# Two-layer hybrid block on one core: a shorter inverse square root, accumulating transfers for the low halves of the head weights, and a new order of the heads' products

## Chip, cores and metric

One core of a Trainium2 chip. The metric is the device time of one execution in microseconds (us); before the change three runs gave 2362.91, 2363.47 and 2366.34, median 2363.47.

## What is computed

Two layers (l = 0, 1), each of three sublayers on x of 512 positions by 1024 channels. All norms are root-mean-square norms with a gain per channel.

```python
for l in range(DEPTH):
    h = swiglu_ffn(rmsnorm(x, ffn1_pre_g[l]), ffn1_w_gu[l], ffn1_w_down[l])
    x = x + 0.5 * rmsnorm(h, ffn1_post_g[l])
    h = mixing_sublayer(rmsnorm(x, mix_pre_g[l]), w_in[l], ...)
    x = x + rmsnorm(h, mix_post_g[l])
    h = swiglu_ffn(rmsnorm(x, ffn2_pre_g[l]), ffn2_w_gu[l], ffn2_w_down[l])
    x = x + 0.5 * rmsnorm(h, ffn2_post_g[l])
```

`swiglu_ffn` is silu(h Wa) * (h Wb) times Wdown with 2816 hidden columns. `mixing_sublayer` multiplies h by a wide `w_in`, runs four branches (a gated MLP over chunks, window means, sparse attention, a causal convolution) and mixes them by gates and `w_out`. `rmsnorm` is h times rsqrt(mean(h*h) + 1e-6) times the gain.

## The kernel before

**Layout and precision.** x is held transposed, eight tiles of 128 channels by 512 positions. Every product of a weight w and a moving tile x is made from rounded high halves and the remainders, as three matmuls: wH·xH, wL·xH, wH·xL (`mm3s`, L244; the `matmul` is L256). So each weight needs two tiles of 128x1024, `wH` and `wL`, four buffers each, and each moving tile an `xH` and an `xL`.

**Weights** (`weights`, L179). A transfer on the SP queue brings the weight to `raw` (L183), the scalar engine (ACT) rounds it to `wH` (L196), and `wL` = raw - wH is made in one of three ways: on VectorE (DVE) by one subtraction (L205), on GpSimd (POOL) in two halves (L205 with `pool`; the first weight of a head has its own form, L189 and L190), or with `far`: ACT writes -wH to `wL` (L198) and a transfer on the POOL queue adds the weight out of DRAM onto it (L199). The mixers' `w_in`, `w_branch` and `w_out` weights use `far`, the feed-forward sublayers' gate, up and down weights use DVE.

**The boundary between two sublayers** (`boundary`, L408; five of them, three behind a feed-forward sublayer and two behind a mixer). The last four output tiles of a sublayer (its tail) and the first four weight columns of the next (its head) are worked in two halves of 256 positions, so that the norm in between overlaps with matmuls. TensorE's order is: tail of the low half, tail of the high half, head of the low half, head of the high half. During the high tail the norm of the low half runs, during the low head that of the high half:

- `compact` (L290): matmuls by a column of ones sum the squares (L296).
- `post_stats` (L346): a chain of small DVE instructions on 128x2 numbers gives the inverse root. Behind a feed-forward sublayer, which works on values not yet scaled by its own pre-norm, this is L357, L358, the eleven of `rsqrt` (L276, three Newton steps) and L360; behind a mixer L362 and the eleven. Two `diag` instructions (L304) put the result on diagonals.
- `spread` (L308): matmuls by ones (L312) bring it to every partition.
- `post_steps` (L377): per channel tile k, DVE scales (L387) and adds to x (L390; odd k on POOL in the high half), ACT makes `xH` (L395). Then eight DVE instructions make `xL` (L401), and ACT and POOL (low half) or DVE (high half) sum the squares for the next pre-norm (L440, L442).

Meanwhile `tail` (L543 and L727) takes each finished tail tile out of PSUM, squares it on ACT (L440) and adds the square to a running sum on DVE or POOL (L442), and `head_weight` (L478 and L563), called after each high tail tile, makes the next head weight; the three of them behind the first have POOL subtract.

**What sets the order.** `after` (L232) keeps a list of work due at a count of TensorE time; `mm3s` looks at it before each step of its own order. So `spread` is asked for 4300 ns of matmuls behind `compact`. The tile framework then schedules each engine's instructions by this program order and by its own estimate of when operands are ready; `pin` (L208) holds chosen ones to program order.

The head's four columns are one call of `mm3s` with `lag=2`:

```python
for ks in (range(n - 1), range(n - 1, n)):
    order += [(k - d, (o, 0)) for k in range(n + lag) for o, d in ((0, 0), (1, lag)) if k - d in ks]
    order += [(k, (0, 1)) for k in ks]
```

that is, for k below 7 the products wH·xH with wL·xH two steps behind, then wH·xL, then the three for k = 7; at each step all four columns. One half of a head is 96 matmuls.

Of the kernel before, what the change touches and what calls it, by code (L numbers as in the profile page):

```python
# [38 lines left out]
ACTIVE = 3  # L39

# [8 lines left out]
class Builder:  # L49
# [129 lines left out]
    def weights(self, src, n, pool=False, ring=False, raw=None, far=False):  # L179

        nc = self.nc
        raw = raw or self.t([P, 1024], F32, "raw", 2)
        nc.sync.dma_start(raw[:, :n], src)  # L183
        if ring:
            hs, ls = [], []
            for i in range(2):
                h, lo = self.ring(), self.ring()
                r = raw[:, i * N:(i + 1) * N]
                nc.scalar.activation(h, r, AF.Copy)  # L189
                nc.gpsimd.tensor_tensor(lo, r, h.bitcast(F32), op=ALU.subtract)  # L190
                hs.append(h)
                ls.append(lo)
            return hs, ls
        h = self.t([P, 1024], F32R, "wH", 4)
        lo = self.t([P, 1024], F32R, "wL", 4)
        self.pin(nc.scalar.activation(h[:, :n], raw[:, :n], AF.Copy))  # L196
        if far:
            nc.scalar.activation(lo[:, :n], raw[:, :n], AF.Copy, scale=-1.0)  # L198
            nc.gpsimd.dma_start(lo[:, :n], src, accum_op=ALU.add)  # L199
            return h, lo  # L200
        e = nc.gpsimd if pool else nc.vector
        w = N if pool and n > N else n
        for c in range(0, n, w):
            c = slice(c, min(c + w, n))
            self.pin(e.tensor_tensor(lo[:, c], raw[:, c], h.bitcast(F32)[:, c], op=ALU.subtract))  # L205
        return h, lo
# [37 lines left out]
    def mm3s(self, jobs, first=True, last=True, lag=0):  # L244

        n = len(jobs[0][1])
        order = []
        for ks in (range(n - 1), range(n - 1, n)):
            order += [(k - d, (o, 0)) for k in range(n + lag) for o, d in ((0, 0), (1, lag)) if k - d in ks]
            order += [(k, (0, 1)) for k in ks]  # L250
        for i, (k, (a, b)) in enumerate(order):
            self.run_due()
            for out, pairs in jobs:
                w, m = pairs[k]
                self.pe += m[b].shape[-1] / 2.4 + 2.5
                self.nc.tensor.matmul(out, w[a], m[b], start=(first and i == 0), stop=(last and i == 3 * n - 1))  # L256
# [12 lines left out]
    def gemms(self, outs, ws, mv, cs=FULL, n=2):  # L269

        for i in range(0, len(outs), n):
            self.mm3s([(o[:, slice(*cs)], self.pairs(w, mv, cs)) for o, w in zip(outs[i:i + n], ws[i:i + n])],
                      lag=2 if n == TAIL else 0)


    def rsqrt(self, y, v):  # L276
        nc = self.nc
        w = v.shape[-1]
        t = self.t([P, 8], F32, "s8", 8)[:, :w]
        nc.vector.tensor_scalar(t.bitcast(I32), v.bitcast(I32), 1, None, op0=ALU.logical_shift_right)  # L280
        nc.vector.tensor_scalar(y.bitcast(I32), t.bitcast(I32), -1.0, float(0x5f3759df), op0=ALU.mult, op1=ALU.add)
        for _ in range(3):
            nc.vector.tensor_tensor(t, y, y, op=ALU.mult)
            nc.vector.scalar_tensor_tensor(t, t, -0.5, v, op0=ALU.mult, op1=ALU.mult)  # L284
            nc.vector.scalar_tensor_tensor(y, t, 1.5, y, op0=ALU.add, op1=ALU.mult)
# [14 lines left out]
    def diag(self, r, cs):  # L300
        c0, c1 = cs[0] // P, cs[1] // P
        dg = self.tmp()
        for c in range(c0, c1):
            self.nc.vector.tensor_scalar(dg[:, c * P:(c + 1) * P], self.ident, r[:, c - c0:c - c0 + 1], None,  # L304
                                         op0=ALU.mult)
# [28 lines left out]
    def pre_stats(self, sub):  # L334
        nc = self.nc
        self.rc = self.t([P, 4], F32, "rc", 2)
# [4 lines left out]
        self.rsqrt(self.rc, ms)  # L341
        dg = self.diag(self.rc, FULL)
# [3 lines left out]
    def post_stats(self, sq, cs, half):  # L346

# [5 lines left out]
        if half:  # L353
            rc = self.rc_prev[:, c0:c0 + w]
            t = self.s8(w)
            nc.vector.tensor_tensor(t, rc, rc, op=ALU.mult)
            nc.vector.scalar_tensor_tensor(ms, ps, 1.0 / D, t, op0=ALU.mult, op1=ALU.mult)  # L357
            nc.vector.tensor_scalar(ms, ms, EPS, None, op0=ALU.add)  # L358
            self.rsqrt(r, ms)
            nc.vector.scalar_tensor_tensor(r, r, 0.5, rc, op0=ALU.mult, op1=ALU.mult)  # L360
        else:
            nc.vector.tensor_scalar(ms, ps, 1.0 / D, EPS, op0=ALU.mult, op1=ALU.add)  # L362
            self.rsqrt(r, ms)
        return self.diag(r, cs)

    def post(self, s, cs, nxt):
# [3 lines left out]
        self.after(4300, lambda: self.step(steps))  # L370
# [74 lines left out]
class FFN:  # L445
# [6 lines left out]
    def gu_weights(self, f, pool=False):  # L452
        return [self.b.weights(self.wgu[self.l, f, ab], 1024, pool) for ab in range(2)]
# [24 lines left out]
    def head_weight(self, i):  # L478
        if i < TAIL:
            self.hw.append(self.b.weights(self.wgu[self.l, i // 2, i % 2], 1024, True, raw=self.b.spare(i)))  # L480
# [20 lines left out]
    def rest(self):  # L501
        b, nc = self.b, self.b.nc
        b.rc_prev = b.rc
# [47 lines left out]
class Mix:  # L551
# [5 lines left out]
    def w(self, i, pool=False, raw=None, far=False):  # L557
        return self.b.weights(self.b.a["w_in"][self.l, i], 1024, pool, raw=raw, far=far)
# [4 lines left out]
    def head_weight(self, i):  # L563
        b = self.b
        if i < TAIL:
            self.hw.append(self.w(i, True, b.spare(i)))
# [220 lines left out]
    def gmlp(self, zv, u):  # L787
# [20 lines left out]
        b.rsqrt(r, ms)  # L808
# [30 lines left out]
    def conv(self):  # L839
# [20 lines left out]
        dg = b.diag(mu, FULL)  # L860
# [192 lines left out]
```

## Time and profile before

| | |
|---|---|
| median of three runs | 2363.47 us |
| the profiled execution's own time | 2364.17 us |
| its span in the profile | 2362.5 us |
| TensorE busy | 2289.8 us (97%) |
| VectorE, ACT, POOL busy | 1231.8, 917.3, 305.8 us |
| moved from DRAM | 270.46 MB, 115 GB/s over the span |

The span runs from the first instruction to the last. Engines are PE (TensorE's matmuls), PEld (its weight loads), DVE, ACT, POOL and SP; L312 is line 312 of the kernel. In a timeline a bracket at the end of a line gives the time that the engine sat idle before it and what ended that.

### The profile page before, as it was taken

Reading aid. Unit: us, or ns where it says so; the run is one execution under the profiler, and the core shown is the slowest. Engines: PE = TensorE matmul, PEld = TensorE weight load, DVE = VectorE, ACT = ScalarE, POOL = GpSimd, SP = SyncE. Lnnn points to the kernel's source line nnn. Section 1 sums busy time; section 2 is a strip of 40 time slices with the busy share of each in tenths; the row PEclk is TensorE's granted clock in tenths of the full one; section 3 lists DMA queues with packets and bytes.
Section 4 is the critical chain, followed back from the end, with each engine's and each line's share of the span. In section 5 each row is a group of like instructions: output and inputs, shape, how many; then the busy total and the mean of one; then the engine's idle time right before and its main releaser. Section 6 shows DMA issues by size and latency. Waiting matters only on the chain.

```text
span 2362.5 us, 28445 instructions
## 1 busy us (share of the span) xinstructions
PE 2289.8 (97%) x11158; PEld 1914.2 (81%) x11158; DVE 1231.8 (52%) x2226; ACT 917.3 (39%) x1375; POOL 305.8 (13%) x341
## 2 busy tenths in 40 slices
PE   8999998999999999999999999989999998999996
PEld 7888888777788888888888888887778888888886
DVE  5334347899433742433573333478985337424335
ACT  4222224564554432222333322345545544322221
POOL 0000003311331300000210000032123213000001
PEclk9999999999999999999999999999999999999998
DMA  5333321867777233333222333327677762333331
GB/s 167 98 106 89 107 89 54 187 143 175 177 163 176 81 100 97 96 101 95 89 83 87 109 96 100 97 64 170 143 178 176 172 160 72 108 92 92 102 93 60
DMA packets 80399, 274.41 MB, mean 116 GB/s; under 512 B 9189, under 2 KB 12937, under 8 KB 80265
## 3 DMA queue, kind: packets, MB, share of 16 engines
q1 hardware_dynamic: 64136, 213.87, 28.8%
q0 software_dynamic: 16128, 58.73, 14.7%
q8 instruction: 87, 1.43, 0.2%
q14 instruction: 48, 0.39, 0.0%
HBM read 270.46 MB, written 2.10 MB: 115 GB/s over the span
## 4 chain that ended last, share of the span: by engine, by line
PE 86%; DVE 8%; DMA 2%; issue 2%; ACT 1%; POOL 0%; SPq 0%; POOLq 0%; ACTq 0%; DVEq 0%
PE mm L256 53%; PE at L256 32%; DMA wL<-in_w_in_dram 1%; DVE x L390 1%; DVE ca L850 1%; DVE xL L401 1%; DVE t L387 1%; DMA raw<-in_w_in_dram 1%; PE st L312 1%; PE st L296 0%; PE at L954 0%; DVE t L304 0%; DVE sc L920 0%; DVE s L284 0%; DMA raw<-in_ffn_w_gu_dram 0%
## 5 line engine op out<-in xcount | busy, mean ns | idle before, releaser
L196 ACT ACTIVATE wH<-raw 128x1024 fp32r<-128x1024 f32 (+1 forms) x394 | 407.4, 1037 | 836.2 <-issue 556.4
L256 PE MATMUL mm<-xH,wH 128*128 128x512 f32 (+1 forms) x1504 | 566.6, 386 | 3.5 <-ACT wH L196 3.5
L256 PE MATMUL mm<-xH,wL 128*128 128x512 f32 (+1 forms) x1504 | 561.3, 383 | 7.9 <-DMA wL<-in_w_in_dram 7.9
L205 DVE TENSOR_TENSOR wL<-raw,wH 128x1024 fp32r<-128x1024 f32 (+1 forms) x272 | 324.2, 1194 | 231.7 <-ACT wH L196 231.6
L256 PE MATMUL mm<-h,wH 128*128 128x512 f32 (+1 forms) x1496 | 407.8, 353 | 0.9 <-DVE t L741 0.9
L256 PE MATMUL mm<-xL,wH 128*128 128x512 f32 (+1 forms) x1504 | 393.0, 379 | 0.0
L256 PEld LDWEIGHTS mm<-xH,wL 128*128 128x128 f32 x1504 | 280.5, 190 | 63.9 <-DMA wL<-in_w_in_dram 10.0
L256 PEld LDWEIGHTS mm<-xH,wH 128*128 128x128 f32 x1504 | 280.8, 191 | 61.2 <-ACT wH L196 4.5
L256 PEld LDWEIGHTS mm<-xL,wH 128*128 128x128 f32 x1504 | 278.2, 189 | 52.9
L256 PE MATMUL at<-xH,wH 128*128 128x512 f32 (+1 forms) x784 | 300.7, 385 | 7.4 <-ACT xH L226 7.2
L256 PEld LDWEIGHTS mm<-h,wH 128*128 128x128 f32 x1496 | 263.2, 188 | 42.2 <-DVE t L741 1.1
L256 PE MATMUL at<-xH,wL 128*128 128x512 f32 (+1 forms) x784 | 297.1, 380 | 0.0
L256 PE MATMUL mm<-h,wL 128*128 128x512 f32 (+1 forms) x748 | 253.8, 354 | 0.0
L256 PE MATMUL at<-h,wH 128*128 128x512 f32 (+1 forms) x776 | 219.6, 366 | 0.0
L256 PE MATMUL at<-xL,wH 128*128 128x512 f32 (+1 forms) x784 | 210.6, 378 | 0.0
L198 ACT ACTIVATE wL<-raw 128x1024 fp32r<-128x1024 f32 x112 | 118.2, 1055 | 185.9 <-PE mm L256 153.5
L256 PEld LDWEIGHTS at<-xH,wH 128*128 128x128 f32 x784 | 148.8, 190 | 37.9 <-ACT xH L226 7.5
L256 PEld LDWEIGHTS at<-xH,wL 128*128 128x128 f32 x784 | 148.4, 189 | 29.3 <-issue 1.4
L256 PEld LDWEIGHTS at<-xL,wH 128*128 128x128 f32 x784 | 147.5, 188 | 27.5
L256 PEld LDWEIGHTS at<-h,wH 128*128 128x128 f32 x776 | 140.4, 188 | 24.6
L256 PEld LDWEIGHTS mm<-h,wL 128*128 128x128 f32 x748 | 140.4, 188 | 20.5
L256 PE MATMUL at<-h,wL 128*128 128x512 f32 (+1 forms) x388 | 136.5, 366 | 0.0
(202 smaller groups left out, 2124.1 us busy)
## 6 DMA issues: line engine op xcount, KB each, us to landing
raw<-in_ffn_w_gu_dram SPq DMA_DIRECT2D x173, 512.0 KB, 3.6
raw<-in_w_in_dram SPq DMA_DIRECT2D x98, 512.0 KB, 6.3
wL<-in_w_in_dram POOLq DMA_DIRECT2D x88, 512.0 KB, 7.2
raw<-in_ffn_w_down_dram SPq DMA_DIRECT2D x64, 448.0 KB, 3.3
raw<-in_ffn_w_down_dram SPq DMA_DIRECT2D x32, 512.0 KB, 3.5
raw<-in_w_branch_dram SPq DMA_DIRECT2D x16, 512.0 KB, 5.2
wL<-in_w_branch_dram POOLq DMA_DIRECT2D x16, 512.0 KB, 7.2
raw<-in_w_out_dram SPq DMA_DIRECT2D x16, 512.0 KB, 5.9
```

Source lines behind the costliest of these rows:

```text
L196: self.pin(nc.scalar.activation(h[:, :n], raw[:, :n], AF.Copy))
L198: nc.scalar.activation(lo[:, :n], raw[:, :n], AF.Copy, scale=-1.0)
L205: self.pin(e.tensor_tensor(lo[:, c], raw[:, c], h.bitcast(F32)[:, c], op=ALU.subtract))
L256: self.nc.tensor.matmul(out, w[a], m[b], start=(first and i == 0), stop=(last and i == 3 * n - 1))
L312: self.nc.tensor.matmul(ps[:, s], self.ones, dg[:, s], start=True, stop=True)
L387: nc.vector.scalar_tensor_tensor(u[:, c], s.o[k][:, c], self.v(s.post[0], s.post[1] + k), pb[:, c], op0=ALU.mult, op1=ALU.mult)
L390: e.tensor_tensor(self.xt[k][:, c], self.xt[k][:, c], u[:, c], op=ALU.add)
L401: nc.vector.scalar_tensor_tensor(self.xl[k][:, c], self.xt[k][:, c], g, self.xh[k].bitcast(F32)[:, c], op0=ALU.mult, op1=ALU.subtract)
L850: nc.vector.scalar_tensor_tensor(a, hp[:, t:t + N], dw(t), a, op0=ALU.mult, op1=ALU.add)
```

## The change

- `rsqrt` starts from one instruction instead of two, makes one Newton step and one step of third order: eight instructions for eleven, with a constant factor of 0.375 left for `diag` to multiply in (or a ninth instruction, in the gated MLP).
- Behind a feed-forward sublayer the pre-norm's own factor is no longer divided out and put back: `pre_stats` keeps 1e-6 times its mean square plus 1e-6 (`ep`, one instruction behind its `diag`), and `post_stats` forms its argument in one instruction. From `compact` to `diag` there are nine small instructions where there were fourteen; behind a mixer nine where there were twelve.
- `spread` is asked for 3400 ns behind `compact` instead of 4300.
- The three later head weights use `far`: ACT writes -wH, the POOL queue issues an adding transfer. POOL's subtractions there are gone, and ACT's copy is pinned.
- The head's products are ordered by `heads`: wH·xH for all k and columns, wL·xH of the first three columns, wH·xL for all, and wL·xH of the last column. The list of due work is looked at before each matmul.

```diff
         if far:
-            nc.scalar.activation(lo[:, :n], raw[:, :n], AF.Copy, scale=-1.0)
+            self.pin(nc.scalar.activation(lo[:, :n], raw[:, :n], AF.Copy, scale=-1.0))
             nc.gpsimd.dma_start(lo[:, :n], src, accum_op=ALU.add)
...
+    def heads(self, jobs):
+        ks = range(KD)
+        js = range(len(jobs))
+        order = [(j, k, 0, 0) for k in ks for j in js]
+        order += [(j, k, 1, 0) for j in js[:-1] for k in ks]
+        order += [(j, k, 0, 1) for k in ks for j in js]
+        order += [(js[-1], k, 1, 0) for k in ks]
+        count = [0] * len(jobs)
+        for j, k, a, b in order:
+            self.run_due()
...
-        nc.vector.tensor_scalar(t.bitcast(I32), v.bitcast(I32), 1, None, op0=ALU.logical_shift_right)
-        nc.vector.tensor_scalar(y.bitcast(I32), t.bitcast(I32), -1.0, float(0x5f3759df), op0=ALU.mult, op1=ALU.add)
-        for _ in range(3):
-            nc.vector.tensor_tensor(t, y, y, op=ALU.mult)
-            nc.vector.scalar_tensor_tensor(t, t, -0.5, v, op0=ALU.mult, op1=ALU.mult)
-            nc.vector.scalar_tensor_tensor(y, t, 1.5, y, op0=ALU.add, op1=ALU.mult)
+        t, h = self.s8(v.shape[-1]), self.s8(v.shape[-1])
+        nc.vector.tensor_scalar(y.bitcast(I32), v.bitcast(I32), -0.5, float(0x5f3759df), op0=ALU.mult, op1=ALU.add)
+        nc.vector.tensor_tensor(t, y, y, op=ALU.mult)
+        nc.vector.scalar_tensor_tensor(t, t, -0.5, v, op0=ALU.mult, op1=ALU.mult)
+        nc.vector.scalar_tensor_tensor(y, t, 1.5, y, op0=ALU.add, op1=ALU.mult)
+        nc.vector.tensor_tensor(t, y, y, op=ALU.mult)
+        nc.vector.tensor_tensor(h, t, v, op=ALU.mult)
+        nc.vector.scalar_tensor_tensor(t, h, -10.0 / 3.0, h, op0=ALU.add, op1=ALU.mult)
+        nc.vector.scalar_tensor_tensor(y, t, 5.0, y, op0=ALU.add, op1=ALU.mult)
+        if exact:
+            nc.vector.tensor_scalar(y, y, CUBIC, None, op0=ALU.mult)
...
         if half:
-            rc = self.rc_prev[:, c0:c0 + w]
-            t = self.s8(w)
-            nc.vector.tensor_tensor(t, rc, rc, op=ALU.mult)
-            nc.vector.scalar_tensor_tensor(ms, ps, 1.0 / D, t, op0=ALU.mult, op1=ALU.mult)
-            nc.vector.tensor_scalar(ms, ms, EPS, None, op0=ALU.add)
-            self.rsqrt(r, ms)
-            nc.vector.scalar_tensor_tensor(r, r, 0.5, rc, op0=ALU.mult, op1=ALU.mult)
+            nc.vector.scalar_tensor_tensor(ms, ps, 1.0 / D, self.ep_prev[:, c0:c0 + w], op0=ALU.mult, op1=ALU.add)
...
-        self.after(4300, lambda: self.step(steps))
+        self.after(3400, lambda: self.step(steps))
...
-            self.hw.append(self.b.weights(self.wgu[self.l, i // 2, i % 2], 1024, True, raw=self.b.spare(i)))
+            self.hw.append(self.b.weights(self.wgu[self.l, i // 2, i % 2], 1024, raw=self.b.spare(i), far=True))
...
-            self.hw.append(self.w(i, True, b.spare(i)))
+            self.hw.append(self.w(i, b.spare(i), True))
```

## Rows read from the trace of the kernel before

**Rows 1.** Waits, in total, of TensorE's matmuls: us, times, longest us.

```profile
PE st L312 <- DVE t L304: 20.3, 9, 3.4
```

**Rows 2.** Windows over both halves of the head, first boundary and sum of five.

```profile
378.80:410.40 31.60, 27.29 (x208) 0.95 0.16 51
...
sum 157.70, PE 132.74; mean PE 26.55
```

**Rows 3.** Timeline of TensorE: sums (L296) and spreads (L312), first and third boundary, end.

```profile
374.14 0.70 PE L312 MATMUL st<-t,ones 128*128 128x256 f32 x2 [1.65 <-DVE t L304]
...
383.81 0.58 PE L296 MATMUL st<-ones,t 128*128 128x1 f32 x4 [1.66 <-DVE t L442]
...
394.48 0.70 PE L312 MATMUL st<-t,ones 128*128 128x256 f32 x2 [1.59 <-DVE t L304]
...
1190.63 1.22 PE L312 MATMUL st<-t,ones 128*128 128x256 f32 x2 [3.14 <-DVE t L304]
...
2348.24 1.19 PE L312 MATMUL st<-t,ones 128*128 128x256 f32 x2 [3.43 <-DVE t L304]
```

**Rows 4.** Timeline of DVE at the first boundary, behind a feed-forward sublayer.

```profile
368.06 0.16 DVE L357 SCALAR_TENSOR_TENSOR s<-st,s 128x2 f32<-128x2 f32 x1 [0.70 <-PE st L296]
...
371.33 1.27 DVE L360 SCALAR_TENSOR_TENSOR s<-s,rc 128x2 f32<-128x2 f32 x1
372.64 1.45 DVE L304 TENSOR_SCALAR t<-ident,s 128x128 f32<-128x128 f32 x2
...
375.67 1.86 DVE L390 TENSOR_TENSOR x<-x,t 128x256 f32<-128x256 f32 x2
...
385.05 6.22 DVE L401 SCALAR_TENSOR_TENSOR xL<-x,vec,xH 128x256 fp32r<-128x256 f32 x7
...
393.74 0.16 DVE L360 SCALAR_TENSOR_TENSOR s<-s,rc 128x2 f32<-128x2 f32 x1
393.94 0.48 DVE L304 TENSOR_SCALAR t<-ident,s 128x128 f32<-128x128 f32 x2
```

**Rows 5.** Line L390, all on DVE: duration ns min/median/max.

```profile
L390 DVE TENSOR_TENSOR x<-x,t x68: 409/419/1523, 375.7 to 2353.6; 128x256 f32<-128x256 f32 x68
```

**Rows 6.** Timeline of POOL at the first boundary.

```profile
371.30 2.51 POOL L205 TENSOR_TENSOR wL<-ca,wH 128x512 fp32r<-128x512 f32 x2 [0.21 <-ACT wH L196]
...
375.90 2.79 POOL L205 TENSOR_TENSOR wL<-raw,wH 128x512 fp32r<-128x512 f32 x2
...
384.93 6.05 POOL L442 TENSOR_TENSOR t<-t,t 128x256 f32<-128x256 f32 x7 [2.27 <-ACT t L440]
```

**Rows 7.** Timeline of DVE at the second boundary, behind a mixer.

```profile
795.28 0.87 DVE L387 SCALAR_TENSOR_TENSOR t<-y,vec,st 128x256 f32<-128x256 f32 x2 [2.17 <-PE st L312]
...
805.48 0.41 DVE L442 TENSOR_TENSOR t<-t,t 128x256 f32<-128x256 f32 x1
```

**Rows 8.** Windows of ACT alone at these two boundaries: length, busy (instructions).

```profile
365.00:391.00 26.00, 12.29 (x25) 0.93 0.14 42
791.00:810.00 19.00, 13.04 (x28) 0.94 0.29 86
```

**Rows 9.** Line L198, ACT's copy of -wH in the mixers: ns min/median/max.

```profile
L198 ACT ACTIVATE wL<-raw x112: 1040/1060/1063, 412.2 to 1925.9; 128x1024 fp32r<-128x1024 f32 x112
```

**Rows 10.** Line L199, the adding transfers in the mixers.

```profile
DMA to landing us min/median/max: 5.1/7.2/10.9
```

**Rows 11.** Windows of TensorE from the head's start to its spread, first and second boundary.

```profile
378.79:394.20 15.41, 11.98 (x84) 0.89 0.23 69
...
800.60:814.10 13.50, 9.31 (x62) 0.87 0.27 79
```

**Rows 12.** Chain that ended last: a dense piece of half-width matmuls.

```profile
2334.97 2.83 PE mm L256 x24
```

**Rows 13.** Windows of TensorE after a spread, third and fifth boundary: busy (matmuls), granted clock.

```profile
1190.00:1193.30 3.30, 2.67 (x10) 0.51 0.23 38
...
1976.00:1979.40 3.40, 3.40 (x31) 1.00 0.28 111
```

## Prediction before the run

> **What bounds the kernel now.** The page's first part shows TensorE busy nearly throughout, so the question is where it isn't. Next the list of waits: of the matmuls' waits the largest total is that of the spreads (L312) for DVE's diagonals, 20.3 us in nine [rows 1]. Then windows over both halves of the head at each boundary: 157.7 us for the five [rows 2]. Dense, a half-width matmul takes 2.83 / 24 = 0.118 us [rows 12], so 192 of them and some 1.5 us for sums and spreads would be 24.2 us, and five of these 121: about 37 us are lost there, 1.5% of the run. The PE timeline of one boundary shows the loss as three waits on DVE: low spread, high sum, high spread [rows 3]. So at a boundary DVE's chain is the bound and TensorE follows; away from the boundaries this change touches next to nothing. Last, DVE's own timeline says why it is slow there: instructions that last 0.16, 0.48 and 0.42 us elsewhere last 1.27, 1.45 and up to 1.52 [rows 4, 5], each time while POOL runs one of its subtractions [rows 6].
>
> **The change part by part, first boundary (behind a feed-forward sublayer; three such).** I follow the start of the high spread, now 394.48, since everything left of the head waits for that or stands behind it.
>
> *Low chain.* Five small instructions fewer; from 393.74 to 393.94 is one link, 0.20 us [rows 4]: 1.0 us. With POOL's subtraction gone L360's place costs 0.16 instead of 1.27 and the diagonals 0.48 instead of 1.45: 2.1 us. DVE is ready 3.1 us sooner. But the spread also needs its place on TensorE: it now waits 1.65 us there, and being due 900 ns sooner moves it some eight matmuls forward, 0.9 us. So it can start 2.6 us sooner, and that is what I take; the wait of 1.65 goes, and the high tail and the head start that much earlier.
>
> *Steps.* Two pairs of L390 like the one at 375.67 take 1.86 us where two at the median are 0.84 [rows 4, 5]: some 1.0 each, 2.1 us with rounding, all beside subtractions. Taken whole; bounds 0 and 2.1.
>
> *Low parts xL.* Seven L401 take 6.22 us beside seven sums of squares on POOL that take 6.05 [rows 4, 6]. Neither is touched: nothing gained.
>
> *High chain.* Five links again: 1.0 us. Total sooner: 2.6 + 2.1 + 1.0 = 5.7 us.
>
> *Added on ACT.* Three copies of 1.06 us [rows 9] in front of, or between, the xH tiles and the last tail tile's square, for which the high sum waits (1.66 us already) [rows 3]. ACT is busy 12.3 of 26 us here [rows 8], so the copies could hide entirely; but they fall in a crowd, since each is tied to the end of a tail tile, and whatever follows on ACT's queue waits. Bounds 0 and 3.2 us; I take two of the three, 2.1, because the second and third stand just ahead of xH tiles and of the square.
>
> *Added transfers.* POOL's queue holds the issue until ACT's copy is done; behind it on POOL stand the square of the next tail tile and the seven sums, all of them later than that. For the second weight: POOL could start at 375.9 [rows 6], plus 1.06, plus 7.2 to land [rows 10] is 384.2. TensorE asks for it after 48 matmuls of the head, 378.8 - 1.65 + 48 x 0.118 = 382.8, plus the wait at the high sum: about in time. With the slowest landing, 10.9, it would be at 387.9, still ahead of the spread at some 390, for which TensorE waits anyway. The last weight's low half is asked for behind 88 of 96. So I cost the transfers at nothing; the cover is that wait. If it goes, a landing of 10.9 costs up to 4 us at a boundary.
>
> *New order of products.* The count of matmuls is the same. Twelve matmuls (k = 7 of three kinds, four columns) are no longer kept back, so xH tiles are asked for every four matmuls, 0.47 us, from the start, rather than slower and with k = 7 last; they come every 0.8 us or so (one L387 and one L390). Bounds: 0 and 1 us; it lies ahead of the high spread, so 0.
>
> *Place of the high spread.* What is queued behind it on TensorE cannot run while it waits. It now stands behind some 84 - 4 = 80 matmuls of the head [rows 11], though it is due after 52 by the old count: the framework's own estimate puts it there. The new count has it due after 41 (9 to the sum, 32 more at 0.109 us each). Each place forward costs 0.118 us while DVE is the bound. Bounds 0 (stays at 80) and 39 places, 4.6 us. I take 10 places, 1.2 us: the estimate sees ten fewer small instructions, but ACT's copies too, which work the other way.
>
> Sum: 5.7 - 2.1 - 1.2 = 2.4 us each, 7.2 us for three.
>
> **Behind a mixer (two).** The low spread has no wait worth the name, so only 0.9 us for its due time. The steps from 795.28 to 805.48 [rows 7] hold 10.2 us; eight L387 at 0.87 a pair, eight L390 at 0.42 and two L401 like such a pair would be 3.5 + 3.4 + 0.9 = 7.8, 2.4 less; I take the 2.1 of the other boundary. The chain loses three links, 0.6. Together 3.6; ACT, busier here (13.0 of 19 us [rows 8]), gives back 2.1. The spread stands behind 62 - 4 = 58 matmuls [rows 11], little above its due place; I leave it. 1.5 us each, 3.0 for two.
>
> **The end and the rest.** After the last sublayer nothing covers the chain: TensorE waits 3.43 us for it [rows 3], and five links are 1.0 us. `pre_stats` is hidden under two full columns; the shorter roots inside the mixers lie beside matmuls; the new `ep` instruction stands behind its diagonals. Nothing for these; if their cover went, three links of 0.2 us a mixer.
>
> Total: 7.2 + 3.0 + 1.0 = 11.2 us. The profiled execution took 2364.17 us, 0.7 above the median: 2353.0, and 2352.3 against the median of 2363.47. I say 2352.
>
> The clock is left out of the sum: in four of five boundaries the granted clock fell to 0.5, that is 1.2 GHz, for a stretch near the stalls. In the third, around a wait of 3.14 us for the high spread [rows 3], 10 matmuls ran in 3.3 us at 0.51, where 31 ran at full clock in 3.4 us of the fifth [rows 13]. Where such a stretch lies behind the spread it costs about 1.5 us, so shorter waits may save up to 6 us over the run and new ones add as much as 7.5.
>
> **Rivals.**
>
> *The stalls go almost wholly.* ACT's copies hide and the spread keeps its place: 5 x 2.1 + 3 x 1.2 = 14.1 us more, 25.3 in all: 2338, and 2332 with the clock stretches gone. For it: ACT is idle half the time. Against: its queue runs in order.
>
> *POOL's squares take over from its subtractions.* POOL still adds two squares of tail tiles in each stretch of steps, at 0.86 us apiece by the seven at 384.93 [rows 6]. If each of these now catches an L390, as a subtraction did, 1.7 of the 2.1 us comes back at every boundary, 8.6 in all, and 2.6 is left: 2361, no difference. For it: the L401 in the trace last 0.89 us beside these sums. Against: there DVE met seven in a row; the two are single, and in the trace both long pairs fall on subtractions. The Trainium skill (SBUF — State Buffer, Who interferes with whom) has a DVE instruction with two SBUF inputs and a GpSimd one that reads SBUF exclude each other wholly, whichever starts first; by that it is no matter what POOL computes, and the sum would be this rival's. The trace agrees as far as the 1.86 and 6.22 us go.
>
> *The spread moves forward on TensorE faster than it is ready (slower).* If the framework puts the high spread at its new due place, 41, 39 matmuls go behind it at the feed-forward boundaries and 17 at the mixers': 4.6 and 2.0 us. With ACT's three copies fully in the way, readiness gains only 5.7 - 3.2 = 2.5 and 3.6 - 3.2 = 0.4. Net 2.1 x 3 + 1.6 x 2 - 1.0 = 8.5 us slower: 2372. It decides when the place moves by more than 2.5 / 0.118 = 21 matmuls at the former, 3 at the latter. For it: due times were shortened by less than the chain only in the low half. Against: until now the framework placed it late.
>
> *It doesn't do what it says.* Due times act only if the framework follows them; with 80 against 52 it already doesn't. Then low and high spread stay where they were, the gain is DVE's alone, and the result lies between the forecast and the first rival.
>
> **How the numbers follow.** About 0.2%, 4.7 us, is what a measurement of this kernel can tell from no change. Forecast, 5 to 20 us gained (2344 to 2358): 0.50, including the case that due times do nothing. Stalls gone, 2331 to 2344: 0.22. POOL's squares or another way to nothing: 0.16. Spread too early, slower by more than 4.7 us: 0.12. So faster 0.72, same 0.16, slower 0.12. The range goes from 2334 to 2364: it leaves out the far end of the first rival and the slower case with part of the null, some 0.2.
>
> **What would show it.** Right: the low spread at the three feed-forward boundaries without its wait; DVE's pairs of L390 near 0.84 us and no instruction on 128x2 above 0.2; 4 to 6 us less from low sum to high spread there before ACT's share; the five head windows summing to 147 or so. Wrong: transfers of low halves as releasers of head matmuls; the square of the last tail tile waiting for ACT's copies for more than 2 us; the high spread's wait above 3 us at most boundaries; windows of 157 or more.

## The result, and the profile of the kernel after

The kernel after took **2332.45 us** (median of four runs, 2331.42 to 2333.25), the kernel before beside it 2363.82: a ratio of 0.9852, 95% interval 0.9836 to 0.9868 (these two medians alone divide to 0.9867, inside it; run again on another chip, the kernel after gave 0.9855). That is 31.4 us faster. The forecast was 2352, with 2334 to 2364 for the range: the direction was right, the size was not, and the time lies just below the range. The profiled execution took 2332.65 us; its span is 2330.9, against 2362.5 before, so 31.6 us are to be found in the trace.

The waits of TensorE's matmuls in the kernel after, in total (us, times, longest us), which answer to [rows 1]:

```profile
PE st L330 <- DVE t L322: 10.5, 6, 2.4
...
PE mm L253 <- DMA wL<-in_w_in_dram: 6.5, 5, 3.8
...
PE st L314 <- DVE t L457: 3.4, 3, 2.8
```

L330 is the spread's matmul (L312 before), L314 that of the sums (L296), L322 `diag` (L304). The spreads' wait for DVE has halved, from 20.3 us in nine to 10.5 in six. Above all, no matmul of a head (L287 now) waits for a transfer; the L253 that do are the mixers' own columns. The windows over both halves of the head, as in [rows 2] (length, busy, matmuls, granted clock):

```profile
376.58:405.33 28.75, 26.29 (x203) 0.94 0.38 95
...
sum 139.97, PE 129.41; mean PE 25.88
```

157.7 us have become 140.0, where some 147 were forecast. TensorE's sums and spreads at the first boundary, then the high spread at the second, then the end, as in [rows 3]:

```profile
367.12 0.61 PE L314 MATMUL st<-ones,t 128*128 128x1 f32 x4
...
371.09 0.59 PE L330 MATMUL st<-t,ones 128*128 128x256 f32 x2
...
381.60 0.50 PE L314 MATMUL st<-ones,t 128*128 128x1 f32 x4
...
387.53 1.22 PE L330 MATMUL st<-t,ones 128*128 128x256 f32 x2 [2.01 <-DVE t L322]
...
805.82 0.70 PE L330 MATMUL st<-t,ones 128*128 128x256 f32 x2 [0.84 <-DVE t L322]
...
2318.21 0.58 PE L314 MATMUL st<-ones,t 128*128 128x1 f32 x4 [2.75 <-DVE t L457]
2321.13 1.22 PE L330 MATMUL st<-t,ones 128*128 128x256 f32 x2 [2.34 <-DVE t L322]
```

The low spread and the high sum have lost their waits; the high spread still has one, and at the first boundary it is longer than before. DVE's timeline at that boundary shows why (answers to [rows 4]):

```profile
373.57 1.00 DVE L405 TENSOR_TENSOR x<-x,t 128x256 f32<-128x256 f32 x2
...
375.55 1.26 DVE L416 SCALAR_TENSOR_TENSOR xL<-x,vec,xH 128x256 fp32r<-128x256 f32 x3
...
379.00 0.75 DVE L405 TENSOR_TENSOR x<-x,t 128x256 f32<-128x256 f32 x2
...
380.01 0.86 DVE L416 SCALAR_TENSOR_TENSOR xL<-x,vec,xH 128x256 fp32r<-128x256 f32 x2
...
381.13 2.23 DVE L416 SCALAR_TENSOR_TENSOR xL<-x,vec,xH 128x256 fp32r<-128x256 f32 x3
383.29 0.15 DVE L375 SCALAR_TENSOR_TENSOR s<-st,rc 128x2 f32<-128x2 f32 x1
383.47 0.52 DVE L294 TENSOR_SCALAR s<-s 128x2 int32<-128x2 int32 x1
384.02 0.16 DVE L295 TENSOR_TENSOR s<-s 128x2 f32<-128x2 f32 x1
384.22 0.59 DVE L296 SCALAR_TENSOR_TENSOR s<-s,s 128x2 f32<-128x2 f32 x1
...
386.65 0.83 DVE L322 TENSOR_SCALAR t<-ident,s 128x128 f32<-128x128 f32 x2
```

And POOL's, as in [rows 6]:

```profile
381.37 5.83 POOL L457 TENSOR_TENSOR t<-t,t 128x256 f32<-128x256 f32 x7 [1.52 <-ACT t L455]
```

The steps' additions (L405) are down to 0.75 to 1.00 a pair. What is slow on DVE now is what runs beside POOL's seven sums of squares: three xL (L416) take 2.23 us, and in the high chain every second instruction takes 0.52 to 0.59 us instead of 0.16. These sums were there before too, but then the high chain came behind them, and now it starts two microseconds after they do.

**Where the 31.6 us came from.** The table takes the starts of the sums and spreads in TensorE's timeline: for each of the five boundaries from the low sum to the low spread, on to the high spread, on to the spread of the next norm's statistics, summed over the five; then from the last low sum to the end of the span; then all the rest. At the first boundary of the kernel after, for example, the second column is 387.53 - 371.09 = 16.4 us.

| us, five boundaries | low sum to low spread | low to high spread | high to next spread | end | rest |
|---|---|---|---|---|---|
| before | 30.1 | 100.2 | 113.4 | 29.7 | 2089.1 |
| after | 20.0 | 85.3 | 116.1 | 25.0 | 2084.5 |
| change | -10.1 | -14.9 | +2.7 | -4.7 | -4.6 |
| forecast | -9.6 | -4.2 | +3.6 | -1.0 | 0 |

The second column of the forecast is 3.1 - 2.1 = 1.0 three times and 2.7 - 2.1 = 0.6 twice, the third its 1.2 three times.

### The profile page after: what moved, and what is told of

Read it like the earlier page. It is cut to its first block, busy times and chain, and to the rows that moved or that the text cites. A ratio compares the mean times of both kernels' runs of the same rounds, so it can differ in the third digit from the quotient of the medians.

```text
span 2330.9 us, 28353 instructions
## 1 busy us (share of the span) xinstructions
PE 2283.6 (98%) x11158; PEld 1909.0 (82%) x11158; DVE 1193.7 (51%) x2144; ACT 927.4 (40%) x1390; POOL 276.6 (12%) x326
## 3 DMA queue, kind: packets, MB, share of 16 engines
q0 software_dynamic: 18288, 66.59, 16.7%
## 4 chain that ended last, share of the span: by engine, by line
PE 85%; DVE 9%; ACT 2%; issue 2%; DMA 1%; POOL 0%; SPq 0%; POOLq 0%; DVEq 0%; ACTq 0%
PE mm L253 49%; PE at L253 31%; DVE ca L865 3%; PE mm L287 2%; PE at L287 1%; DMA wL<-in_w_in_dram 1%; DVE sc L935 1%; DVE t L402 1%; DVE m L934 1%; PE st L330 1%; PE st L314 1%; DVE x L405 1%; DVE xL L416 1%; ACT wH L197 0%; DVE t L646 0%
## 5 line engine op out<-in xcount | busy, mean ns | idle before, releaser
L253 PE MATMUL mm<-xH,wL 128*128 128x512 f32 x1344 | 525.9, 392 | 6.5 <-DMA wL<-in_w_in_dram 6.5
L253 PE MATMUL mm<-xH,wH 128*128 128x512 f32 x1344 | 530.5, 396 | 1.6 <-DVE t L756 1.3
L253 PE MATMUL mm<-h,wH 128*128 128x512 f32 (+1 forms) x1496 | 409.2, 354 | 0.3 <-DVE t L756 0.3
L253 PE MATMUL mm<-xL,wH 128*128 128x512 f32 x1344 | 359.0, 389 | 0.0
L253 PEld LDWEIGHTS mm<-xH,wL 128*128 128x128 f32 x1344 | 253.4, 189 | 61.7 <-DMA wL<-in_w_in_dram 9.4
L253 PEld LDWEIGHTS mm<-xH,wH 128*128 128x128 f32 x1344 | 253.3, 188 | 58.5 <-issue 4.2
L253 PEld LDWEIGHTS mm<-h,wH 128*128 128x128 f32 x1496 | 263.8, 188 | 41.8 <-DVE t L756 0.5
L253 PEld LDWEIGHTS mm<-xL,wH 128*128 128x128 f32 x1344 | 252.5, 188 | 52.6
L253 PE MATMUL at<-xH,wH 128*128 128x512 f32 x704 | 277.1, 395 | 7.3 <-ACT xH L223 6.7
L253 PE MATMUL at<-xH,wL 128*128 128x512 f32 x704 | 274.0, 391 | 0.0
L253 PE MATMUL mm<-h,wL 128*128 128x512 f32 (+1 forms) x748 | 252.4, 352 | 0.0
L253 PE MATMUL at<-h,wH 128*128 128x512 f32 (+1 forms) x776 | 219.6, 366 | 0.0
L199 ACT ACTIVATE wL<-raw 128x1024 fp32r<-128x1024 f32 x122 | 128.6, 1054 | 176.9 <-PE mm L253 144.9
L253 PE MATMUL at<-xL,wH 128*128 128x512 f32 x704 | 187.8, 389 | 0.0
L253 PEld LDWEIGHTS at<-xH,wH 128*128 128x128 f32 x704 | 132.9, 189 | 37.6 <-ACT xH L223 7.0
L253 PEld LDWEIGHTS at<-h,wH 128*128 128x128 f32 x776 | 140.4, 188 | 24.6
L253 PEld LDWEIGHTS mm<-h,wL 128*128 128x128 f32 x748 | 140.4, 188 | 20.3
L253 PEld LDWEIGHTS at<-xH,wL 128*128 128x128 f32 x704 | 132.7, 188 | 29.3 <-issue 1.4
L253 PEld LDWEIGHTS at<-xL,wH 128*128 128x128 f32 x704 | 132.2, 188 | 27.5
L253 PE MATMUL at<-h,wL 128*128 128x512 f32 (+1 forms) x388 | 136.5, 366 | 0.0
```

The costliest lines, as they stand in the source:

```text
L199: self.pin(nc.scalar.activation(lo[:, :n], raw[:, :n], AF.Copy, scale=-1.0))
```

## The experiments

Every kernel ran beside the kernel before on its own chip, where that took 2366 to 2367 us in place of 2363.8; so ratios are compared rather than times.

**Each part of the change undone alone** (and the other three kept). For the subtractions on POOL (in short; for the three later head weights alone):

```diff
-            self.pin(nc.scalar.activation(lo[:, :n], raw[:, :n], AF.Copy, scale=-1.0))
-            nc.gpsimd.dma_start(lo[:, :n], src, accum_op=ALU.add)
+            for c in range(0, n, N):
+                c = slice(c, min(c + N, n))
+                self.pin(nc.gpsimd.tensor_tensor(lo[:, c], raw[:, c], h.bitcast(F32)[:, c], op=ALU.subtract))
```

> The changed kernel with the three later head weights split by POOL's subtractions again, the rest as changed. Theory: DVE was slowed at the boundaries by POOL's subtractions, and ACT's copies hide; then some 3 to 4 us come back at each of five boundaries: 2344 to 2352, with L405 on DVE again up to 1.5 us and small instructions above 1 us. Rival: ACT's copies cost the 2.1 us a boundary that the prediction took; then taking them away gives back 10 us of it, 2334 to 2340. Second rival: the transfers are not what brought the gain at all; within 3 us of 2332.

Measured: 2364.21 us, 0.9988 (0.9976 to 1.0). The whole gain is gone, more than expected. From low to high spread it needs 108.7 us, 8.6 more than the kernel before. DVE's additions at the first boundary (L410 there):

```profile
374.51 1.35 DVE L410 TENSOR_TENSOR x<-x,t 128x256 f32<-128x256 f32 x1
...
376.56 2.87 DVE L410 TENSOR_TENSOR x<-x,t 128x256 f32<-128x256 f32 x2
...
381.20 2.06 DVE L410 TENSOR_TENSOR x<-x,t 128x256 f32<-128x256 f32 x2
```

and POOL beside them:

```profile
373.03 2.55 POOL L201 TENSOR_TENSOR wL<-ca,wH 128x512 fp32r<-128x512 f32 x2 [0.15 <-ACT wH L197]
...
376.42 2.74 POOL L201 TENSOR_TENSOR wL<-raw,wH 128x512 fp32r<-128x512 f32 x2
...
381.70 2.71 POOL L201 TENSOR_TENSOR wL<-raw,wH 128x512 fp32r<-128x512 f32 x2 [0.16 <-ACT wH L197]
```

With the chain shorter, the steps run into all three subtractions instead of two: a chain that ends sooner only meets the same obstacle sooner. The end is 4.5 us later too (see POOL's DRAIN below). Head matmuls also wait 12.3 us in all for wH, which they did not in the kernel after.

The old order of products (`mm3s` with its lag of two for the head):

```diff
-            (self.heads if n == TAIL else self.mm3s)(jobs)
+            self.mm3s(jobs, lag=2 if n == TAIL else 0)
```

> The changed kernel with the head's products in the old order (k = 7 kept back, low halves two steps behind) and due work looked at every four matmuls; the rest as changed. Theory: the order gains little by itself, but with the old one the low halves are asked for after three steps, before the transfers have landed: matmuls of the head wait for wL, 3 to 5 us at each boundary, 2346 to 2358. Rival: the transfers land early enough in any order, 2330 to 2336.

Measured: 2352.29 us, 0.9936 (0.992 to 0.9953), as expected. Its waits of TensorE, and the one at the first boundary:

```profile
PE mm L253 <- DMA wL<-in_w_in_dram: 13.6, 6, 4.7
PE mm L253 <- DMA wL<-in_ffn_w_gu_dram: 12.4, 3, 4.5
```

```profile
384.76 0.58 PE L253 MATMUL mm<-xH,wL 128*128 128x256 f32 x1 [4.21 <-DMA wL<-in_w_in_dram]
```

Low halves out of DRAM come too late for an order that asks for all of them early. The prediction had 384.2 for this landing; TensorE starts at 384.76, at a boundary whose low sum comes 1.2 us later than in the kernel before. The waits are not the whole loss: in or just behind each of the five the granted clock is 0.50 for 6.8 us, where the kernel after has two such stretches of 3.4 us at its boundaries.

The old root (`rsqrt`, `diag`) and the old argument of it (`pre_stats`, `post_stats`), fourteen and twelve small instructions instead of nine; `post_stats` in short:

```diff
-        self.rsqrt(r, ms)
-        return self.diag(r, cs, CUBIC * (0.5 if half else 1.0))
+            rc = self.rc_prev[:, c0:c0 + w]
+            t = self.s8(w)
+            nc.vector.tensor_tensor(t, rc, rc, op=ALU.mult)
+            nc.vector.scalar_tensor_tensor(ms, ps, 1.0 / D, t, op0=ALU.mult, op1=ALU.mult)
...
+        return self.diag(r, cs)
```

> The changed kernel with the old inverse root and the old argument of post_stats (fourteen and twelve small instructions), 3400 ns kept. Theory: links of 0.20 us on DVE's path, five in the high and less in the low half: 1.0 to 2.0 us at three boundaries, 0.6 to 1.2 at two, 1.0 at the end: 2337 to 2342, and the low spread waits again by up to 1 us. Rival: the shorter chain only moves a wait; 2331 to 2334.

Measured: 2345.97 us, 0.9908 (0.9891 to 0.9925), dearer than expected: low sum to high spread grows from 105.3 to 112.1 us (6.8), the end by 2.2, and the rest by 6.9, in part by a stretch of the slow clock of 6.8 us in the second mixer; from the high spread to the next it is 2.9 us less. What remains of the rest wasn't followed up.

The old due time of the spread:

```diff
-        self.after(3400, lambda: self.step(steps))
+        self.after(4300, lambda: self.step(steps))
```

> The changed kernel with the spread due 4300 ns behind the sum again. Theory: the low spread no longer waits for DVE, so its due place counts: 0.9 us at five boundaries, 2335 to 2338. Rival: the framework places it by its own estimate; within 2 us of 2332.

Measured: 2341.69 us, 0.9897 (0.9881 to 0.9914): more than either side expected. Low sum to high spread is 104.8 us, the same as the 105.3 of the kernel after; the loss is behind the high spread, 127.3 us against 116.1. The windows from low sum to high spread at the first and second boundary (length, busy, matmuls in brackets), in the kernel after:

```profile
367.10:387.45 20.35, 17.96 (x144) 1.00 0.58 131
783.75:805.77 22.02, 20.82 (x167) 1.00 0.64 164
```

with the old due time:

```profile
369.20:390.75 21.55, 17.29 (x136) 1.00 0.54 123
785.75:806.15 20.40, 17.98 (x147) 1.00 0.72 177
```

and in the kernel before:

```profile
367.40:394.45 27.05, 21.71 (x161) 0.94 0.14 40
789.40:814.15 24.75, 20.42 (x153) 0.93 0.28 85
```

So the earlier due time doesn't make DVE ready sooner; it has TensorE do 8 and 20 more matmuls while it waits anyway, 3 x 8 + 2 x 20 = 64 of 0.118 us, 7.6 us. The other 3.6 are less than the clock can account for: with the old due time a stretch of 3.4 us at 0.50, 1.2 GHz, follows the high spread at all five boundaries, in the kernel after at two, and three more dense ones would cost 1.7 us each.

**Parts alone**, put into the kernel before: the adding transfers, the order, the chain (the diffs above, reversed).

> The kernel before with the adding transfers for the three later head weights as the only change (old order, old root, 4300 ns). Theory, after the undo runs: taking POOL's subtractions away frees DVE, but the old order asks for low halves three steps into the head, before they land, so matmuls wait for the transfers and most is given back: 2355 to 2370. Rival: freeing DVE alone is the gain, 2335 to 2350.

Measured: 2350.28 us, 0.9927 (0.9912 to 0.9941), 16.7 us below the kernel before beside it. That is better than the theory expected and within the gain that the rival gave, although the waits for low halves came (28.4 us in all). 4.5 us of the gain are the end's, by POOL's DRAIN (below).

> The kernel before with the head's new order of products as the only change. Theory: with POOL's subtractions DVE is as late as before, and the order asks for xH tiles sooner, so it gains nothing: 2360 to 2372. Rival: the order alone gives the 20 us that undoing it cost: 2342 to 2350.

Measured: 2372.76 us, 1.0017 (1.0002 to 1.0033): the order alone gains nothing.

> The kernel before with the shorter inverse root and argument as the only change. Theory: links of 0.20 us on the path, 5 or 3 a half, and 1.0 at the end: 2355 to 2361. Rival: 2362 to 2366, since the spread's place on TensorE does not move.

Measured: 2352.2 us, 0.9937 (0.9925 to 0.9949), 14.8 us below the kernel before beside it, where 3 to 9 were expected. The profiled execution, the slowest of five, has 8.9 of them, 5.3 from low sum to low spread; where the others lie wasn't followed up.

**Two parts together**, adding transfers and order, with the old chain and due time:

> The kernel before with the adding transfers and the new order of products together, the old root and the old due time kept. If the four parts only add up, undoing the chain (13.5 us) and the due time (9.2) from the kernel after gives 2355, and the two alone from the kernel before (16.7 less and 5.8 more) give 2356. If the new order needs the adding transfers and pays only with them, by taking away the waits for the last low half that the old order shows, it is 2340 to 2349.

Measured: 2349.59 us, 0.9932 (0.9918 to 0.9946), the same as the transfers alone. The order pays 0.8% with the short chain and the early due time, but nothing here: it takes the waits for wL from 28.4 us in all to 7.5, and in their place the spreads wait 18.5 us for DVE instead of 3.4, since the long chain is not ready any sooner. The parts are worth 0.73, -0.17 and 0.63% alone and 1.36, 0.84 and 0.56% as the last one added; they don't add up, since each wait that goes uncovers the next.

**What ACT's copies cost.** First doubled, for the three late weights of each head:

```diff
         if far:
+            if self.pinned:
+                self.pin(nc.scalar.activation(lo[:, :n], raw[:, :n], AF.Copy, scale=-1.0))
             self.pin(nc.scalar.activation(lo[:, :n], raw[:, :n], AF.Copy, scale=-1.0))
```

> The kernel after, with the copy of -w made twice on ACT for each of the three late weights of a head: 15 more ACT instructions of some 1.04 us, each in the same place of ACT's queue as the one it doubles, and each adding transfer asked for that much later. By the prediction's price, two of three copies in the way, this costs 2.1 us a boundary, 10.5 us in all: about 2343 us. By the theory formed since, that these copies hide in ACT's idle time and that the transfers have time to spare, it costs under 3 us: 2331 to 2336, and still no head matmul waits for a transfer of wL.

Measured: 2341.76 us, 0.9898 (0.9882 to 0.9915): in all the prediction's price, not that of the later theory. The five boundaries take 229.3 us against 221.4, 1.6 more each. The rest of the profiled execution, the slowest of four, is 5.9 us longer, 3.4 of them by the clock in the mixers. No head matmul waits for a transfer, but those that wait for ACT's xH and wH go from 1.6 to 8.5 us in all. ACT's last square of the tail (L457 there) and the last of the copies ahead of it, and then TensorE:

```profile
381.27 1.04 ACT L201 ACTIVATE wL<-raw 128x1024 fp32r<-128x1024 f32 x1
...
383.42 0.40 ACT L457 ACTIVATE t<-y 128x256 f32<-128x256 f32 x1
```

```profile
384.52 0.57 PE L316 MATMUL st<-ones,t 128*128 128x1 f32 x4
...
389.65 0.70 PE L332 MATMUL st<-t,ones 128*128 128x256 f32 x2 [2.31 <-DVE t L324]
```

But a second set of copies needn't cost what the first did. So they were left out, with a plain transfer in place of the adding one (the low halves of these 15 weights then hold the weight itself, and their share of the products is not the reference's):

```diff
+        if far and self.pinned:
+            nc.gpsimd.dma_start(lo[:, :n], src)
+            return h, lo
```

> The kernel after, with ACT's copies of -w left out for the three late weights of a head, and a plain transfer of the weight on POOL's queue in place of the adding one: these 15 low parts hold the weight itself, so the output leaves out what the low parts bring. The number and size of the transfers and all else stay. If the first three copies of a boundary cost what the second three did in the kernel with doubled copies (1.6 us a boundary), or the prediction's 2.1, the boundaries are 8 to 10 us shorter here than in the kernel after on the same chip. If the first three hide in ACT's idle time, it is within 3 us of that kernel; the low spread to high spread stretch behind a feed-forward sublayer then stays near 16.4 us, against 20.4 in the kernel before.

> The kernel after once more, beside the one without the copies on the same chip. The kernel before stood at 2367 us in the later runs against 2364 in the first, so this one should stand at 2332 to 2337; both theories on the copies are read from the difference to it.

Measured: 2335.29 us without the copies (2330.84 to 2337.07; 0.9863, 0.9846 to 0.988) and 2332.37 for the kernel after (0.9855, 0.9836 to 0.9875). The boundaries take 220.6 us without, 221.4 with. Without copies the first boundary's high sum and spread are

```profile
381.64 0.58 PE L317 MATMUL st<-ones,t 128*128 128x1 f32 x4
...
389.25 1.14 PE L333 MATMUL st<-t,ones 128*128 128x256 f32 x2 [2.77 <-DVE t L325]
```

so the sum comes 9.2 us behind the low spread (at 372.41) instead of 10.5, and the spread no sooner: 16.8 instead of 16.4. The three copies delay the high sum by 1.3 us, but without them the high chain is not ready any earlier: DVE's order is another there, with six xL in a row beside POOL's sums.

```profile
381.41 4.87 DVE L419 SCALAR_TENSOR_TENSOR xL<-x,vec,xH 128x256 fp32r<-128x256 f32 x6
```

So this run doesn't price the copies with all else in its place. The kernel after itself says why they hide behind a feed-forward sublayer: its high sum is through at 382.10, and DVE is busy with xL until 383.29, when the high chain starts. Behind a mixer DVE does wait for ACT's last square, and the copies cost 1.6 us up to the high spread; TensorE uses them for matmuls that it then has done (167 from low sum to high spread, 151 without copies), and behind the spread 1.4 us come back. The first three hide, the next three don't.

**What POOL's remaining sums cost.** The low half's squares and sums moved behind the high half's xL:

```diff
-        for k in range(KD):
-            self.sq_add(self.sqx, self.xt[k], cs, k == 0, first)
-            yield 0
+        if not first:
+            for h in HALVES:
+                for k in range(KD):
+                    self.sq_add(self.sqx, self.xt[k], h, k == 0, h == HALVES[0])
+                    yield 0
```

> The kernel after, with the low half's squares and their seven sums on POOL moved from behind the low half's xL to behind the high half's, so that POOL adds nothing while DVE runs the last xL of the low half and the high chain. The theory, that a POOL instruction of two inputs beside a DVE one still slows DVE there (three xL in 2.23 us instead of 1.26, eight links in 3.36 instead of 1.77), expects some 2.5 us a boundary behind a feed-forward sublayer and 0 to 2.5 behind a mixer: 2320 to 2327, with no instruction of the high chain on 128x2 above 0.2 us. The rival: the sum over both halves now comes after the high steps, and the spread of the next norm, hidden until now, turns into a wait: 2332 to 2342.

Measured: **2319.2 us**, 0.9801 (0.9787 to 0.9816): faster than both kernels, 13 us below the kernel after. Its high chain on DVE at the first boundary:

```profile
382.83 1.26 DVE L416 SCALAR_TENSOR_TENSOR xL<-x,vec,xH 128x256 fp32r<-128x256 f32 x3
...
384.19 0.17 DVE L294 TENSOR_SCALAR s<-s 128x2 int32<-128x2 int32 x1
...
385.77 0.48 DVE L322 TENSOR_SCALAR t<-ident,s 128x128 f32<-128x128 f32 x2
```

the high spread that follows, and its five head windows:

```profile
386.72 0.59 PE L330 MATMUL st<-t,ones 128*128 128x256 f32 x2
```

```profile
sum 124.70, PE 122.33; mean PE 24.47
```

and its waits:

```profile
PE st L330 <- DVE t L322: 2.3, 1, 2.3
...
PE mm L287 <- DMA wL<-in_ffn_w_gu_dram: 0.6, 1, 0.6
```

No spread waits for DVE at any boundary (the one of 2.3 us is the end's), and the heads are within 4 us of the 121 that the prediction gave for dense ones. The rival, a wait at the next norm's spread, did not come. The one head matmul that waits for a low half's transfer, 0.6 us, shows that their cover begins to run out.

The boundaries are 13.0 us shorter than in the kernel after, and not all of that is POOL's. Behind the three feed-forward sublayers it is 9.6 us: the high sum comes as before, 10.5 us behind the low spread, and DVE's xL and high chain are faster; but 3 us of it are two stretches of the slow clock that don't come here. Behind the two mixers it is 3.4 us, and there ACT is the cause: the edit moves ACT's eight squares of the low half as well, which in the kernel after stood ahead of the last tail tile,

```profile
798.06 2.24 ACT L455 ACTIVATE t<-x 128x256 f32<-128x256 f32 x7
```

and the high sum comes 11.4 us behind the low spread instead of 14.3.

**What the end's saving hangs on.** POOL's last instruction, a DRAIN, is much shorter after the change. The rows are those of the kernel's last line by engine (count: ns min/median/max, first and last start); before, and after:

```profile
L1048 POOLq DRAIN  x3: 40/102/7945, 2353.7 to 2362.2; - x3
```

```profile
L1063 POOLq DRAIN  x3: 40/93/2682, 2326.7 to 2330.6; - x3
```

The kernels with POOL's subtractions, which issue 112 transfers on POOL's queue, had the long one; those with 127 transfers the short one. To tell the two apart, 15 transfers were taken from the mixers' weights:

```diff
-        w = self.w(i, far=True)
+        w = self.w(i, far=not 6 <= i < 14 - self.l)
```

> The kernel after, with 15 of the mixers' 112 adding transfers (8 in one, 7 in the other) taken back to a copy and a subtraction on DVE, so that POOL's queue issues 112 transfers as in the kernel before instead of 127; the heads' weights stay as they are after the change. POOL's last instruction at the end lasted 7.95 us in each kernel with POOL's subtractions of the heads' low halves and 2.68 in each without. If the number of adding transfers sets it, it is 7.9 here again and the end 3 to 5 us later; if the subtractions do, it stays at 2.7. The rest of the time should move by under 5 us either way, since both the copies and the subtractions lie beside the mixers' matmuls: 2329 to 2338 with the short one, 2332 to 2342 with the long one.

Measured: 2343.64 us, 0.9904 (0.9888 to 0.992), and

```profile
L1063 POOLq DRAIN  x3: 40/93/7948, 2332.0 to 2340.5; - x3
```

POOL's subtractions have nothing to do with it, since this kernel has none; the transfers on POOL's queue do. The five boundaries are those of the kernel after (221.4 us), the end is 4.5 us later, and 5.3 go to the rest, where DVE now subtracts for 15 of the mixers' weights. That last part was above what was expected.

## Why the prediction was wrong in size

**Low chain: right.** Low sum to low spread shortened by 10.1 us over the five, 9.6 forecast. The spread's wait is gone, and its place moved by about as much as the due time said.

**The copies on ACT: the step that failed.** The prediction took 2.1 us a boundary off for ACT's copies, 10.5 us in all, because two of three stand ahead of xH tiles and the last square. They do, and they delay that square. Behind a feed-forward sublayer it didn't end the chain, xL on DVE did; behind a mixer it did end it, and TensorE had other matmuls to do meanwhile. Without the copies the five boundaries are 0.8 us shorter, not 10.5. Of its bounds, 0 and 3.2, the lower one held; the 2.1 that was taken is near what three more copies cost, 1.6. Half of the missing 20.4 us (31.6 less 11.2) is this term; 3.7 are the end, 4.6 the rest of the kernel, which was put at nothing, and 1.6 small differences of the other columns.

**Steps and high chain: right in their sum, by luck.** Steps and links come to 3.1 x 3 + 2.7 x 2 = 14.7 us; measured from low to high spread were 14.9, 3.9 apiece behind the feed-forward sublayers and 1.6 behind the mixers. The parts are others. In the kernel before the high chain of the first boundary starts at

```profile
391.19 0.15 DVE L357 SCALAR_TENSOR_TENSOR s<-st,s 128x2 f32<-128x2 f32 x1
```

that is 17.05 us behind the low spread, and in the kernel after 383.29 - 371.09 = 12.2: 4.9 us sooner, where the steps were to give 2.1. The eight additions are 2.7 us shorter in all. The eight xL, put at nothing, are 2.4 shorter, since five of them now stand ahead of POOL's sums, where before seven ran beside them; that order comes with the adding transfers (alone in the kernel before, they bring the first xL of this boundary from 10.2 to 3.5 us behind the low spread). And the high chain with its diagonals, which was to be 1.0 us shorter, is 1.0 longer, 4.2 us instead of 3.2, because it now runs beside those sums. So the sign that no instruction on 128x2 would take above 0.2 us failed.

**The end: mis-sized.** 4.7 us instead of 1.0. The chain itself gave only 0.2 from the last low sum to the last high spread: it is 1.1 us shorter from the high sum on, as forecast, but that sum comes 0.9 us later than before. The last spread to the end fell from 14.2 to 9.7 us by the DRAIN, which the prediction didn't look at, though its 7.9 us stood in the trace.

**The clock: left out, and it gave something.** In the kernel before four stretches in the mixers ran at 0.50 of the full clock, 3.4 us each and dense, 6.8 us lost. One of them, and the only one that the kernel after has there (length, busy, matmuls, clock):

```profile
490.30:493.70 3.40, 3.40 (x10) 0.50 1.05 201
```

```profile
530.90:537.70 6.80, 5.76 (x14) 0.50 0.75 200
```

That is 3.4 us of the 4.6 in the rest. It differs between executions: the kernel after, run again, has one more such stretch of 3.4 us in the second mixer. At the boundaries both kernels have two such stretches at or behind a high spread, so there it made no difference; the kernel before has two more ahead of one, where TensorE then waits for DVE anyway.

**The place of the high spread: right in the sum, not in its parts.** The matmuls between low sum and high spread fell from 161 to 144 behind a feed-forward sublayer, 17 places where 10 were taken, and rose from 153 to 167 behind a mixer, where none was. Net 3 x 17 - 2 x 14 = 23 places, 2.7 us, as measured (3.6 forecast).

**Transfers and order: right at nothing, but not free of each other.** The landings were in time as worked out. The order was put at 0 us by itself; but the transfers rest on it: without it the matmuls' waits for low halves rise from 6.5 to 26.0 us, the clock falls at each of them, and the kernel is 20 us slower.

**The rivals.** The result is in size the first one (2332 with the clock stretches gone), and its first reason held: the copies hide. Its others didn't quite: the spread lost places, and the DRAIN made that up, so that the size agrees is luck. The second, POOL's squares in the place of its subtractions, did not happen at the additions (0.75 to 1.00 a pair) but did a stage later, at the high chain; the run that moved those sums, and ACT's squares with them, is 13 us faster. The Trainium skill (SBUF — State Buffer, Who interferes with whom) says that the port pair which DVE and GpSimd share is an exclusive lock, and that the order of issue decides which of them is blocked. The trace agrees in the pattern: beside sums of 5.83 / 7 = 0.83 us, one DVE instruction takes 0.5 to 0.6 us, the next 0.16. The slower rival did not come: the spread moved forward by 17 places, short of its 21, behind a feed-forward sublayer, and back behind a mixer. Due times were followed by the low spread: with the old one it comes 0.94 us later at each boundary.

## What to carry to other kernels

Before work added to an engine is priced, find out whether that engine's last instruction is what ends the chain; a delay that another wait outlasts costs nothing, up to the point where it doesn't. When two engines slow one another, ask not only how long the slower runs but what it will stand beside once the chain has moved: moving POOL's remaining sums, and ACT's squares for them, gave another 13 us. And where a sum comes out right, look at its terms: here wrong ones cancelled. Parts that each remove a wait aren't worth the sum of their values alone.

## What the runs showed that was not expected

POOL's closing DRAIN took 7.95 us in kernels with 112 transfers on its queue and 2.68 with 127; with 15 of the 127 plain instead of adding, 2.40:

```profile
L1066 POOLq DRAIN  x3: 40/93/2395, 2324.9 to 2328.9; - x3
```

More transfers, a shorter drain: what in the queue sets it stays open, since only these two counts were run.

Instructions on 128x2 numbers, the smallest on DVE, lose nearly as much to POOL's sums as large ones: 0.52 and 0.59 us instead of 0.16, where an xL takes 0.89 (6.22 / 7) instead of 0.42 (1.26 / 3).

An adding transfer of 512 KB on POOL's queue takes longer than a plain one: the heads' feed-forward weights landed in 7.4 us (median of nine) in the kernel after, and in 4.7 in the kernel without the copies, where the transfer is plain.
